# S5 tables moved from GpSimd to VectorE and ScalarE, background PSUM banks behind the LayerNorm lead, epilogue steps moved to VectorE

## The chip, the core and the metric

One core of one Trainium2 chip runs the whole program in one launch. The metric is the device time of one execution in microseconds (us). Before the change three runs took 3293.79, 3299.25 and 3299.61 us; their median is 3299.25 us.

## The reference, cut to what matters

Two decoder blocks of two layers each run one after the other on 256 tokens of width 2048, all in float32:

```python
# block 1
x = LN(ALPHA*x + short_conv_mixer(x))      # w_in 2048x6144, 3-tap causal conv, w_out
x = LN(ALPHA*x + conv_ffn(x))              # w_up 2048x11264, 3-tap conv + bias, silu(g)*u, w_down
x = LN(ALPHA*x + diff_attention(x, k, v))
x = LN(ALPHA*x + conv_ffn(x))
# block 2
h = h + ab_layer(rmsnorm(h))               # dilated attention, gated linear attention
h = h + cd_layer(rmsnorm(h))               # S5 state space layer, gated recurrence
return rmsnorm(h, final_g)

# inside cd_layer, from the parameters alone (no activations):
dt = exp(log_dt); mag = exp(lam_re*dt); ang = lam_im*dt
ab = mag*cos(ang) + 1j*mag*sin(ang)
bb = ((ab - 1)/lam) * b                    # complex; lam, b, c are parameters
# x_t = ab*x_{t-1} + bb u_t ;  y_t = Re(c x_t) + d*u_t
```

The S5 layer is evaluated with tables that depend on the parameters alone (powers of `ab`, rotations, input and output matrices), so they can be made at any time before the last layer.

## The kernel before, in words

**Units.** All weights are streamed from HBM in units of 128 x 1024 numbers (`_units`). For every unit SyncE loads `raw` (3 buffers), ScalarE rounds it to `whi` (`hi_to`, 4 buffers), VectorE makes the rest `wlo = raw - whi` (`lo_to`, 4 buffers), and TensorE multiplies with both halves: 8 matmuls of 512 columns with `whi` (the activations `xs` lie as high and low parts side by side) and 8 of 256 columns with `wlo`. A regular tile of 128 output channels (`mm_tile`) has two units; two units in a row take the halves in turned order (`st["kind"]`), so that the second begins with `wlo`. The result lies in a PSUM bank as two parts of 256 columns.

**Order.** The order of every engine's instructions is written out by the program. `before_unit` emits the load five units ahead and the rounding two ahead; `after_unit` emits `wlo` and then one step of every waiting epilogue (`pending`, `advance`) and of the background generators (`run_bg`): `bg` always, `slow` only while `st["quiet"]` is false. A `yield n` in a background generator lets n units pass. All engines work off their queues in order.

**PSUM.** Three banks with the tag `mm` (pool `pmm`) serve regular tiles, four with the tag `bg` (pool `pbg`) serve background work, one serves statistics. `mm_side` and `mm_lead` work on four tiles at once and take banks of both pools. `merge` frees the bank of a regular tile: ScalarE copies one part to `mt`, and a step later VectorE adds the other (L539).

**Lead.** After a LayerNorm the next product begins before the normalisation is done. `mm_lead` runs two groups of four tiles (16 units) on the unnormalised sum with extra columns: the first group on the four `bg` banks, the second on the three `mm` banks and one `bg` bank. `LayerNorm.apply` (`feed`) meanwhile makes the normalised `hres`, and from it pair after pair of 128-row blocks of `xs`: `high` on ScalarE, `low` on VectorE (L743). What is left of `feed` is emitted in one go behind the lead. The epilogue of a lead tile is `normed`: ScalarE copies four extra columns to `uv`, a step later VectorE adds two of them (L767) and applies mean and deviation (L768, L769), and ScalarE adds the bias. The next regular tile takes the first `mm` bank, which that L768 frees. There are four leads: up of the first FFN, q, up of the second FFN, ab.

**FFN.** `ffn` runs three times an up part (44 pairs of tiles in all) and a down part. The epilogue of an up tile (`epi_up`) merges into `pad`, then `conv3` makes the three taps: the first on ScalarE (an activation with scale and bias), and after a `yield` two on VectorE (L849, L850); then comes SiLU or the product with the gate, and the split into high and low parts.

**Tables.** `s5_tables` is a `slow` generator. GpSimd does nearly all its arithmetic: after a preparation on 32-column rows, eight iterations, each with a table of rotations (36 small operations), a matrix `ba` (six operations of 512 columns), a matrix `ca` (six of 640, one more for the sign, two copies of 512), eight transposes of `ba` on TensorE (tag `bg`, evicted by ScalarE) and 16 matmuls for `s5k`. One iteration's yields add up to 32 units. `LayerNorm.add` sets `quiet` from output tile 4 of the last product on; the end of the lead clears it. `open_b`, in the lead of q, finishes whatever is left.

Of the kernel before, what the change touches and what calls it, by code (L numbers as in the profile page):

```python
# [25 lines left out]
OP = mybir.AluOpType  # L26
# [120 lines left out]
def kernel(ctx: ExitStack, tc: tile.TileContext, A, out, dbg=None, upto=99):  # L147
# [445 lines left out]
    class LayerNorm:  # L593
# [53 lines left out]
        def add(self, m, base):  # L647
# [15 lines left out]
            st["quiet"] = True  # L663
            if m >= 8:
                st["hold"] = True
# [206 lines left out]
    def epi_xv(i):  # L872
        def f(ps):
# [5 lines left out]
            yield from conv3(cur["y", i], pad, [P("a_conv", j * 16 + i) for j in range(3)])  # L879
# [83 lines left out]
    def s5_tables():  # L963
# [7 lines left out]
        def cmul(dr, di, ar, ai, br, bi, eng, u1, u2):  # L971
            eng.tensor_mul(u1, ar, br)
            eng.tensor_mul(u2, ai, bi)
            eng.tensor_sub(dr, u1, u2)
            eng.tensor_mul(u1, ar, bi)
            eng.tensor_mul(u2, ai, br)
            eng.tensor_add(di, u1, u2)
# [10 lines left out]
        G.tensor_mul(abr, mag, cs)  # L988
        G.tensor_mul(abi, mag, sn)
        G.tensor_mul(t1, lr, lr)  # L990
        G.tensor_mul(t2, li, li)
        G.tensor_add(t1, t1, t2)
        yield 4
        V.reciprocal(inv, t1)
        yield 2
        G.tensor_scalar(nr, abr, -1.0, None, op0=OP.add)
        G.tensor_mul(t1, nr, lr)
        G.tensor_mul(t2, abi, li)
        G.tensor_add(t1, t1, t2)
        G.tensor_mul(cor, t1, inv)  # L1000
        G.tensor_mul(t1, abi, lr)
        G.tensor_mul(t2, nr, li)
        G.tensor_sub(t1, t1, t2)
        G.tensor_mul(coi, t1, inv)
        yield 1
        G.tensor_mul(t1, mag, mag)
        G.tensor_mul(mag4, t1, t1)
        G.memset(pa[:, 0, :, 0], 1.0)
        G.memset(pa[:, 1, :, 0], 0.0)
        G.tensor_copy(pa[:, 0, :, 1], abr)  # L1010
        G.tensor_copy(pa[:, 1, :, 1], abi)
        for a, b in ((1, 1), (2, 1), (2, 2)):
            cmul(pa[:, 0, :, a + b], pa[:, 1, :, a + b], pa[:, 0, :, a], pa[:, 1, :, a],
                 pa[:, 0, :, b], pa[:, 1, :, b], G, t1, t2)
        for j in range(4):
            G.tensor_copy(pd[:, :, :, j], pa[:, :, :, 3 - j])
# [3 lines left out]
        cmul(*ph, cs, sn, cs, sn, G, t1, t2)  # L1020
        cmul(pq[:, 0, 0], pq[:, 1, 0], *ph, *ph, G, t1, t2)
        for j in range(5):
            cmul(pq[:, 0, j + 1], pq[:, 1, j + 1], pq[:, 0, j], pq[:, 1, j], pq[:, 0, j], pq[:, 1, j], G, t1, t2)
        yield 1
# [15 lines left out]
        for i in range(8):  # L1040
# [3 lines left out]
            G.tensor_copy(d0[:, :, 1:], mag4[:, p4].unsqueeze(2).to_broadcast([128, 4, 63]))  # L1044
            for k in range(6):
# [3 lines left out]
                cmul(rot[:, 0, :, n:2 * n], rot[:, 1, :, n:2 * n], rot[:, 0, :, :n], rot[:, 1, :, :n],  # L1049
                     fr, fi, G, v1, v2)  # L1050
            yield 3
            cr, ci = (z[:, p4].unsqueeze(2).to_broadcast([128, 4, 16]) for z in (cor, coi))
            w1, w2 = u1[:, :, 0, :16], u2[:, :, 0, :16]
            for r in range(2):
                G.tensor_mul(w1, cr, bc[:, r])
                G.tensor_mul(w2, ci, bc[:, 1 - r])
                for ps_, cs_ in half:
                    (G.tensor_add if r else G.tensor_sub)(bd[ps_, r, :, cs_], w1[ps_], w2[ps_])
# [880 lines left out]
```

## Time and profile before

| | |
|---|---|
| median of three runs | 3299.25 us |
| the profiled execution | 3297.42 us, of which span 3295.6 us |
| mean granted TensorE clock | 0.987 |
| TensorE (PE) busy | 3201.6 us, 97% |
| VectorE (DVE) busy | 2338.4 us, 71% |
| ScalarE (ACT) busy | 1718.4 us, 52% |
| GpSimd (POOL) busy | 827.4 us, 25% |
| DMA | 599.31 MB, mean 182 GB/s |

The span is the time from the first to the last instruction; 1.8 us of the execution lie outside it. Idle time matters on the engine that bounds the kernel, so the page is read together with what ended each wait of that engine. PEclk, the granted clock, is 1.00 at 2.4 GHz and 0.50 at 1.2 GHz.

### The profile page before, as it was taken

The page shows a single profiled execution, that of the slowest core. Times are in us where ns is not written, and L with a number is a line of the kernel's source. Part 1 is how long each engine was busy: PE and PEld are TensorE (multiplying, and loading weights), DVE is VectorE, ACT ScalarE, POOL GpSimd, SP SyncE. Part 2 cuts the span into 40 slices and gives each one's busy share as a digit, 9 for nine tenths or more (in the row PEclk, how much of TensorE's full clock was granted, in tenths as well). Part 3 has the DMA queues.
Part 4 walks back from the last instruction along what each step waited for, and adds up shares of the span by engine and source line. Part 5 has one row for each costly group of instructions (what it writes and reads, how often), then busy time and mean ns, then how long its engine had stood idle before and what let it go on. Part 6 is the DMA issues. An engine that isn't in the chain of part 4 may idle for free.

```text
span 3295.6 us, 51934 instructions
## 1 busy us (share of the span) xinstructions
PE 3201.6 (97%) x18966; PEld 2834.0 (86%) x18966; DVE 2338.4 (71%) x3529; ACT 1718.4 (52%) x2664; POOL 827.4 (25%) x1081
## 2 busy tenths in 40 slices
PE   9989989999999999999999999999989999999998
PEld 8878978788888898887988888888878888899887
DVE  6657886677766787667877676677877666688765
ACT  5544565445545564555655455455564565444754
POOL 4565342455650036241200000000300001121102
PEclk9999999999999999999999999999999999999999
DMA  7656646666656655555556666666544555775454
GB/s 219 195 175 196 189 145 195 185 200 184 202 184 200 187 171 182 158 159 163 171 171 191 188 187 190 191 186 190 163 146 151 161 179 183 226 258 167 151 180 154
DMA packets 258960, 599.31 MB, mean 182 GB/s; under 512 B 38128, under 2 KB 137072, under 8 KB 258704
## 3 DMA queue, kind: packets, MB, share of 16 engines
q1 hardware_dynamic: 256320, 588.38, 58.3%
q0 software_dynamic: 2208, 7.37, 0.7%
q8 instruction: 150, 2.46, 0.3%
q14 instruction: 106, 0.87, 0.1%
q10 hardware_dynamic: 176, 0.23, 0.0%
HBM read 578.04 MB, written 17.83 MB: 181 GB/s over the span
## 4 chain that ended last, share of the span: by engine, by line
PE 73%; DVE 11%; DMA 4%; ACT 4%; issue 3%; POOL 2%; SPq 1%; DVEq 0%; ACTq 0%; POOLq 0%
PE mm L314 43%; PE mm L308 22%; DVE wlo L244 6%; ACT whi L201 3%; DMA raw<-in_cd_dram 1%; PE ml L1383 1%; DVE h L849 1%; SPq L219 1%; DMA raw<-in_up_dram 1%; PE mm L401 1%; PE mm L402 0%; PE mm L400 0%; PE mm L311 0%; PE s5k L1083 0%; DMA raw<-in_ab_dram 0%
## 5 line engine op out<-in xcount | busy, mean ns | idle before, releaser
L244 DVE TENSOR_TENSOR wlo<-raw,whi 128x1024 fp32r<-128x1024 f32 (+3 forms) x1083 | 1366.0, 1264 | 728.8 <-ACT whi L201 700.0
L201 ACT ACTIVATE whi<-raw 128x1024 fp32r<-128x1024 f32 (+3 forms) x1083 | 1119.6, 1038 | 566.0 <-PE mm L314 205.0
L314 PE MATMUL mm<-xs,whi 128*128 128x512 f32 x5264 | 1304.2, 397 | 22.6 <-DVE pad L768 10.4
L314 PEld LDWEIGHTS mm<-xs,whi 128*128 128x128 f32 x5264 | 970.4, 190 | 218.2 <-issue 20.0
L308 PEld LDWEIGHTS mm<-xs,wlo 128*128 128x128 f32 x5264 | 676.5, 190 | 47.3 <-DVE wlo L244 17.6
L308 PE MATMUL mm<-xs,wlo 128*128 128x256 f32 x5264 | 694.6, 283 | 15.2 <-DVE wlo L244 15.1
L314 PE MATMUL mm<-glu,whi 128*128 128x512 f32 x1380 | 343.2, 395 | 9.7 <-DVE pad L539 9.7
L314 PEld LDWEIGHTS mm<-glu,whi 128*128 128x128 f32 x1380 | 253.5, 190 | 58.6 <-issue 11.4
L201 ACT ACTIVATE h<-pad,par 128x256 f32<-128x256 f32 x176 | 104.9, 600 | 328.1 <-DVE pad L539 328.0
L201 ACT ACTIVATE mt<-mm 128x256 f32<-128x256 f32 x337 | 124.9, 371 | 196.8 <-PE mm L314 179.9
L689 POOL TENSOR_TENSOR ln_s<-rf 128x256 f32<-128x256 f32 x2 | 2.1, 1055 | 828.8 <-DVE rf L645 828.8
L308 PEld LDWEIGHTS mm<-glu,wlo 128*128 128x128 f32 x1408 | 188.2, 193 | 17.9 <-DVE wlo L244 7.7
L308 PE MATMUL mm<-glu,wlo 128*128 128x256 f32 x1408 | 192.9, 285 | 6.5 <-DVE wlo L244 6.5
L426 PE MATMUL mm<-xs,wlo 128*128 128x258 f32 (+1 forms) x512 | 145.4, 284 | 4.9 <-DVE wlo L244 4.8
L424 PE MATMUL mm<-xs,whi 128*128 128x260 f32 (+1 forms) x512 | 145.9, 285 | 0.7 <-ACT whi L201 0.5
L428 PE MATMUL mm<-xs,whi 128*128 128x256 f32 (+1 forms) x512 | 144.4, 282 | 0.0
L426 PEld LDWEIGHTS mm<-xs,wlo 128*128 128x128 f32 (+1 forms) x512 | 94.8, 185 | 7.5 <-DVE wlo L244 7.1
L850 DVE SCALAR_TENSOR_TENSOR h<-pad,par,h 128x256 f32<-128x256 f32 x176 | 94.2, 535 | 6.3
L424 PEld LDWEIGHTS mm<-xs,whi 128*128 128x128 f32 (+1 forms) x512 | 94.9, 185 | 1.7 <-ACT whi L201 0.7
L849 DVE SCALAR_TENSOR_TENSOR h<-pad,par,h 128x256 f32<-128x256 f32 x176 | 93.3, 530 | 4.0 <-ACT h L201 4.0
L1091 POOL DMA_DIRECT2D s5b<-s5km x8 | 4.4, 554 | 362.7 <-ACT s5km L201 362.7
L428 PEld LDWEIGHTS mm<-xs,whi 128*128 128x128 f32 (+1 forms) x512 | 94.8, 185 | 0.3
(622 smaller groups left out, 3706.3 us busy)
## 6 DMA issues: line engine op xcount, KB each, us to landing
raw<-in_up_dram SPq DMA_DIRECT2D x320, 512.0 KB, 4.3
raw<-in_ab_dram SPq DMA_DIRECT2D x98, 512.0 KB, 3.9
raw<-in_a_in_dram SPq DMA_DIRECT2D x88, 512.0 KB, 4.5
raw<-in_cd_dram SPq DMA_DIRECT2D x88, 512.0 KB, 4.5
raw<-in_down_dram SPq DMA_DIRECT2D x72, 512.0 KB, 3.8
raw<-in_down_dram SPq DMA_DIRECT2D x168, 128.0 KB, 2.6
raw<-in_down_dram SPq DMA_DIRECT2D x48, 448.0 KB, 4.0
raw<-in_up_dram SPq DMA_DIRECT2D x128, 128.0 KB, 3.1
```

Source lines behind the costliest of these rows:

```text
L201: nc.scalar.activation(dst, src, func, **k)
L219: nc.sync.dma_start(r[:, c:c + nk * m], w[t, :, k0:k0 + nk, :].rearrange("p k n -> p (k n)"))
L244: V.tensor_sub(lo[:, c:c + step], r[:, c:c + step], hi[:, c:c + step].bitcast(F32))
L308: PE.matmul(ps[:m, :T], lo[:, c:c + m], x[:, kx, :T], start=False, stop=last, skip_group_check=True)
L314: PE.matmul(ps[:m, :], hi[:, c:c + m], x[:, kx, :], start=first, stop=last, skip_group_check=True)
L401: PE.matmul(ps[b], xhi, wlo[:, :, k, :], start=False, stop=False, skip_group_check=True)
L424: PE.matmul(p[:, :4 + T], hi[:, w], xt[:, k, PAD - 4:PAD + T], start=k == 0, stop=False, skip_group_check=True)
L426: PE.matmul(p[:, 2:4 + T], lo[:, w], xt[:, k, PAD - 2:PAD + T], start=False, stop=False, skip_group_check=True)
L428: PE.matmul(p[:, 4:4 + T], hi[:, w], xt[:, k, PAD + T:], start=False, stop=k == KT - 1, skip_group_check=True)
L849: V.scalar_tensor_tensor(dst, pad[:, 1:T + 1], w[1], dst, op0=OP.mult, op1=OP.add)
L850: V.scalar_tensor_tensor(dst, pad[:, 2:T + 2], w[2], dst, op0=OP.mult, op1=OP.add)
L1383: PE.matmul(ps[:, 2 * b + hd, :], Kf[:, s], rhs, start=b + hd == 0, stop=b + hd == 2, skip_group_check=True)
```

## The change

Five edits:

1. The first two regular tiles behind each lead take a bank of the background pool instead of one of the three `mm` banks.
2. `normed` reads the extra columns on VectorE straight from PSUM, with one copy and one addition in its first step; the ScalarE copy and a `yield` go.
3. `conv3` makes its first tap on VectorE, and its `yield` goes, so that all three taps follow the merge in one step.
4. The arithmetic of `s5_tables` moves from GpSimd to VectorE, in small steps with a yield behind every one to six operations; plain copies, the sign of `ca` and the two wide copies go to ScalarE. Memsets, the sine arguments and the DMA issues stay on GpSimd. The `ca` part now stands behind the transposes and the write of the first table. One iteration still has 32 units of yields.
5. `quiet` is set from output tile 8 on instead of 4.

The core of the diff:

```diff
-    def mm_tile(x, epi, n_units=2, koff=0, whole=False, now=False):
-        ps = pmm.tile([128, 512], F32, tag="mm", name="mm")
+    def mm_tile(x, epi, n_units=2, koff=0, whole=False, now=False, bank=(pmm, "mm")):
+        ps = bank[0].tile([128, 512], F32, tag=bank[1], name="mm")
...
-        for e in epis[SIDE if ln is None else LEAD * SIDE:]:
-            mm_tile(x, e)
+        for i, e in enumerate(epis[SIDE if ln is None else LEAD * SIDE:]):
+            mm_tile(x, e, bank=(pbg, "bg") if ln is not None and i < 2 else (pmm, "mm"))
...
-            st["quiet"] = True
             if m >= 8:
-                st["hold"] = True
+                st["hold"] = st["quiet"] = True
...
             e = lnp.tile([128, 6], F32, tag="uv", name="uv", bufs=4)
-            S.activation(e[:m, :4], ps[:m, :4], AF.Copy)
-            yield
+            V.tensor_copy(e[:m, :2], ps[:m, :2])
+            V.tensor_add(e[:m, 4:], e[:m, :2], ps[:m, 2:4])
             while not self.ready:
                 yield
-            V.tensor_add(e[:m, 4:], e[:m, :2], e[:m, 2:4])
...
     def conv3(dst, pad, w, bias=0.0):
-        S.activation(dst, pad[:, 0:T], AF.Identity, scale=w[0], bias=bias)
-        yield
+        V.tensor_scalar(dst, pad[:, 0:T], w[0], bias, op0=OP.mult, op1=OP.add)
...
+        def cmul(dr, di, ar, ai, br, bi, u1, u2, n=3):
+            ops = ((V.tensor_mul, u1, ar, br), (V.tensor_mul, u2, ai, bi), (V.tensor_sub, dr, u1, u2),
+                   (V.tensor_mul, u1, ar, bi), (V.tensor_mul, u2, ai, br), (V.tensor_add, di, u1, u2))
+            for i, (f, d, x, y) in enumerate(ops):
+                f(d, x, y)
+                if i % n == n - 1:
+                    yield 1
...
-                cmul(rot[:, 0, :, n:2 * n], rot[:, 1, :, n:2 * n], rot[:, 0, :, :n], rot[:, 1, :, :n],
-                     fr, fi, G, v1, v2)
-            yield 3
+                yield from cmul(rot[:, 0, :, n:2 * n], rot[:, 1, :, n:2 * n], rot[:, 0, :, :n], rot[:, 1, :, :n],
+                                fr, fi, v1, v2, 6 if n < 8 else 3 if n < 16 else 2)
...
-            cmul(ba[:, 0], ba[:, 1], ar, ai, br, bi, G, u1[:, :, :4], u2[:, :, :4])
-            yield 8
-            ar, ai = (pa[:, r, p4].unsqueeze(3).to_broadcast([128, 4, 5, 32]) for r in range(2))
-            br, bi = (cd[:, r].unsqueeze(2).to_broadcast([128, 4, 5, 32]) for r in range(2))
-            cmul(ca[:, 0], ca[:, 1], ar, ai, br, bi, G, u1, u2)
-            G.tensor_scalar(ca[:, 1], ca[:, 1], -1.0, None, op0=OP.mult)
-            for r, u in enumerate((u1, u2)):
-                G.tensor_copy(u[:, :, :4], bd[:, r].unsqueeze(2).to_broadcast([128, 4, 4, 32]))
+            yield from cmul(ba[:, 0], ba[:, 1], ar, ai, br, bi, u1[:, :, :4], u2[:, :, :4], 1)
             for r in range(2):
-                if not r:
-                    yield 2
                 ps = pbg.tile([128, 4, 128], F32, tag="bg", name="s5t")
                 for a in range(4):
                     PE.transpose(ps[:, a, :], ba[:, r, a].rearrange("p j h -> p (j h)"), ident)
                 yield 1
                 S.activation(bt[:, :, r, :], ps, AF.Copy)
             nc.sync.dma_start(s5_a[i], ta)
-            yield 12
+            ar, ai = (pa[:, r, p4].unsqueeze(3).to_broadcast([128, 4, 5, 32]) for r in range(2))
+            br, bi = (cd[:, r].unsqueeze(2).to_broadcast([128, 4, 5, 32]) for r in range(2))
+            yield from cmul(ca[:, 0], ca[:, 1], ar, ai, br, bi, u1, u2, 1)
+            copy(ca[:, 1], ca[:, 1], -1.0)
+            yield 1
+            for r, u in enumerate((u1, u2)):
+                copy(u[:, :, :4], bd[:, r].unsqueeze(2).to_broadcast([128, 4, 4, 32]))
+                yield 1
+            yield 1
             ps = pbg.tile([128, 4, 128], F32, tag="bg", name="s5k")
...
```

`copy` is a ScalarE activation with `AF.Copy`. The preparation's 17 operations and ten complex products on 32 columns, and the eight operations of 64 columns that make `bd` in each iteration, move from `G` to `V` in the same way.

## Rows read from the trace of the kernel before

**Rows 1.** The page, part 1: busy time, share of the span, instructions.
```profile
PE 3201.6 (97%) x18966; PEld 2834.0 (86%) x18966; DVE 2338.4 (71%) x3529; ACT 1718.4 (52%) x2664; POOL 827.4 (25%) x1081
```

**Rows 2.** TensorE's waits, longest first: total us, times, longest us.
```profile
PE mm L308 <- DVE wlo L244: 21.6, 13, 3.4
...
PE mm L314 <- DVE pad L539: 9.7, 4, 4.2
PE s5t L1075 <- POOL s5ba L974: 9.6, 1, 9.6
```

**Rows 3.** The windows view: length, busy us of each engine, clock, DMA.
```profile
442.40:1194.50 752.10, 725.26 (x4144) 635.91 (x4145) 539.11 (x719) 381.80 (x582) 315.63 (x429) 0.98 0.62 188
1655.70:2354.80 699.10, 696.17 (x3984) 611.96 (x3985) 486.69 (x719) 362.25 (x539) 26.89 (x25) 0.99 0.62 185
...
679.70:861.60 181.90, 176.08 (x1010) 154.14 (x1009) 129.43 (x171) 96.50 (x155) 84.03 (x114) 0.98 0.61 188
1867.70:2034.90 167.20, 167.20 (x961) 146.81 (x960) 114.66 (x176) 92.14 (x145) 0.00 (x0) 1.00 0.62 186
```

**Rows 4.** Instructions in order of time, 478 to 486 us: start, duration, wait.
```profile
478.78 1.29 POOL L974 TENSOR_TENSOR s5ba<-s5u,s5u 128x512 f32<-128x512 f32 x1
478.80 2.35 DVE L244 TENSOR_TENSOR wlo<-raw,whi 128x1024 fp32r<-128x1024 f32 x1 [1.68 <-ACT whi L201]
...
481.08 1.27 DVE L849 SCALAR_TENSOR_TENSOR h<-pad,par,h 128x256 f32<-128x256 f32 x1
...
485.80 0.62 PE L308 MATMUL mm<-xs,wlo 128*128 128x256 f32 x3 [3.36 <-DVE wlo L244]
```

**Rows 5.** TensorE's table work by line, 442.4 to 1194.5 us: busy us, mean ns.
```profile
L1083 PE MATMUL s5k<-s5ca,s5u 128*128 128x128 f32 x112 | 13.6, 275 | 0.0
L1075 PE MATMUL s5t<-ident,s5ba 128*128 128x128 f32 x48 | 7.2, 272 | 0.0
```

**Rows 6.** VectorE's groups by line and form: busy us, mean ns.
```profile
L1764 DVE TENSOR_SCALAR hg<-vz,lb 128x256 f32<-128x256 f32 x8 | 3.7, 458 | 0.0
...
L1373 DVE TENSOR_TENSOR qt<-hg 128x512 f32<-128x512 f32 x4 | 2.7, 681 | 0.0
L1765 DVE TENSOR_SCALAR hg<-hg 128x256 f32<-128x256 f32 x8 | 2.7, 337 | 0.6 <-PE m L1402 0.3
L1245 DVE TENSOR_TENSOR sm<-sm,lamf 128x1 f32<-128x1 f32 x16 | 2.5, 156 | 0.3
```

**Rows 7.** TensorE's first regular tile behind each lead, in order of time.
```profile
442.41 3.75 PE L314 MATMUL mm<-xs,whi 128*128 128x512 f32 x8 [5.21 <-DVE pad L768]
...
1249.53 3.75 PE L314 MATMUL mm<-xs,whi 128*128 128x512 f32 x8 [3.94 <-DVE qT L768]
...
1655.68 3.75 PE L314 MATMUL mm<-xs,whi 128*128 128x512 f32 x8 [5.21 <-DVE pad L768]
...
2410.30 3.75 PE L314 MATMUL mm<-xs,whi 128*128 128x512 f32 x8 [4.98 <-DVE vz L768]
```

**Rows 8.** The end of three leads on ScalarE, VectorE and TensorE, in order of time.
```profile
1252.01 1.89 DVE L743 TENSOR_TENSOR xs<-hres,xs 128x512 fp32r<-128x512 f32 x3
...
1643.08 1.57 ACT L201 ACTIVATE h<-pad,par 128x256 f32<-128x256 f32 x3
...
1646.16 1.23 DVE L244 TENSOR_TENSOR wlo<-raw,whi 128x1024 fp32r<-128x1024 f32 x1 [4.09 <-ACT whi L201]
...
1657.62 1.13 ACT L201 ACTIVATE xs<-hres 128x512 fp32r<-128x512 f32 x2
...
1658.84 1.89 DVE L743 TENSOR_TENSOR xs<-hres,xs 128x512 fp32r<-128x512 f32 x3
...
1662.08 3.85 PE L314 MATMUL mm<-xs,whi 128*128 128x512 f32 x16
...
2413.11 2.46 DVE L527 SCALAR_TENSOR_TENSOR xs<-hres,par,xs 128x256 fp32r<-128x256 f32 x6
```

**Rows 9.** The windows view of the stretch behind the wait for `s5ba`.
```profile
197.00:207.30 10.30, 5.77 (x19) 5.00 (x20) 3.01 (x3) 1.54 (x2) 9.85 (x12) 0.50 0.01 3
```

More of the change, by code (lines that the diff above doesn't have):

```diff
@@ L878, in f @@
             cur["y", i] = ep.tile([128, T], F32, tag="c2", name="c2")
-            yield from conv3(cur["y", i], pad, [P("a_conv", j * 16 + i) for j in range(3)])
+            conv3(cur["y", i], pad, [P("a_conv", j * 16 + i) for j in range(3)])
         return f
@@ L969, in s5_tables, with copy @@
         lr, li, ld = P("lam_re", 0, 32), P("lam_im", 0, 32), P("log_dt", 0, 32)
[L971 to L977, printed above, removed]
+        def copy(dst, src, scale=1.0):
+            S.activation(dst, src, AF.Copy, scale=scale)
+        def cmul(dr, di, ar, ai, br, bi, u1, u2, n=3):
[5 more added lines that the diff above has]
+                    yield 1
         yield 20
@@ L987, in s5_tables @@
         yield 1
[L988 to L993, printed above, removed]
-        V.reciprocal(inv, t1)
-        yield 2
[L996 to L1002, printed above, removed]
@@ L1003, in s5_tables @@
-        G.tensor_sub(t1, t1, t2)
-        G.tensor_mul(coi, t1, inv)
-        yield 1
-        G.tensor_mul(t1, mag, mag)
-        G.tensor_mul(mag4, t1, t1)
+        V.tensor_mul(abr, mag, cs)
+        V.tensor_mul(abi, mag, sn)
+        V.tensor_mul(t1, lr, lr)
+        V.tensor_mul(t2, li, li)
+        yield 1
+        V.tensor_add(t1, t1, t2)
+        V.reciprocal(inv, t1)
+        V.tensor_scalar(nr, abr, -1.0, None, op0=OP.add)
+        yield 1
+        V.tensor_mul(t1, nr, lr)
+        V.tensor_mul(t2, abi, li)
@@ L1008, in s5_tables @@
+        V.tensor_add(t1, t1, t2)
+        yield 1
+        V.tensor_mul(cor, t1, inv)
+        V.tensor_mul(t1, abi, lr)
+        V.tensor_mul(t2, nr, li)
+        yield 1
+        V.tensor_sub(t1, t1, t2)
+        V.tensor_mul(coi, t1, inv)
+        yield 1
+        V.tensor_mul(t1, mag, mag)
+        V.tensor_mul(mag4, t1, t1)
         G.memset(pa[:, 0, :, 0], 1.0)
         G.memset(pa[:, 1, :, 0], 0.0)
-        G.tensor_copy(pa[:, 0, :, 1], abr)
-        G.tensor_copy(pa[:, 1, :, 1], abi)
+        copy(pa[:, 0, :, 1], abr)
@@ L1012, in s5_tables @@
+        copy(pa[:, 1, :, 1], abi)
+        yield 1
         for a, b in ((1, 1), (2, 1), (2, 2)):
-            cmul(pa[:, 0, :, a + b], pa[:, 1, :, a + b], pa[:, 0, :, a], pa[:, 1, :, a],
-                 pa[:, 0, :, b], pa[:, 1, :, b], G, t1, t2)
+            yield from cmul(pa[:, 0, :, a + b], pa[:, 1, :, a + b], pa[:, 0, :, a], pa[:, 1, :, a],
+                            pa[:, 0, :, b], pa[:, 1, :, b], t1, t2)
         for j in range(4):
-            G.tensor_copy(pd[:, :, :, j], pa[:, :, :, 3 - j])
+            copy(pd[:, :, :, j], pa[:, :, :, 3 - j])
@@ L1017, in s5_tables @@
         yield 1
         pq = bgp.tile([128, 2, 6, 32], F32, tag="s5pq", name="s5pq", bufs=1)
-        cmul(*ph, cs, sn, cs, sn, G, t1, t2)
-        cmul(pq[:, 0, 0], pq[:, 1, 0], *ph, *ph, G, t1, t2)
+        yield from cmul(*ph, cs, sn, cs, sn, t1, t2)
+        yield from cmul(pq[:, 0, 0], pq[:, 1, 0], *ph, *ph, t1, t2)
         for j in range(5):
-            cmul(pq[:, 0, j + 1], pq[:, 1, j + 1], pq[:, 0, j], pq[:, 1, j], pq[:, 0, j], pq[:, 1, j], G, t1, t2)
-        yield 1
+            yield from cmul(pq[:, 0, j + 1], pq[:, 1, j + 1], pq[:, 0, j], pq[:, 1, j], pq[:, 0, j], pq[:, 1, j],
+                            t1, t2)
@@ L1043, in s5_tables @@
             p4 = slice(4 * i, 4 * i + 4)
-            G.tensor_copy(d0[:, :, 1:], mag4[:, p4].unsqueeze(2).to_broadcast([128, 4, 63]))
+            copy(d0[:, :, 1:], mag4[:, p4].unsqueeze(2).to_broadcast([128, 4, 63]))
             for k in range(6):
@@ L1078, in s5_tables @@
             nc.sync.dma_start(s5_a[i], ta)
-            yield 12
+            ar, ai = (pa[:, r, p4].unsqueeze(3).to_broadcast([128, 4, 5, 32]) for r in range(2))
+            br, bi = (cd[:, r].unsqueeze(2).to_broadcast([128, 4, 5, 32]) for r in range(2))
+            yield from cmul(ca[:, 0], ca[:, 1], ar, ai, br, bi, u1, u2, 1)
+            copy(ca[:, 1], ca[:, 1], -1.0)
+            yield 1
+            for r, u in enumerate((u1, u2)):
+                copy(u[:, :, :4], bd[:, r].unsqueeze(2).to_broadcast([128, 4, 4, 32]))
+                yield 1
+            yield 1
             ps = pbg.tile([128, 4, 128], F32, tag="bg", name="s5k")
@@ L1091, in s5_tables @@
             nc.gpsimd.dma_start(s5_b[i][:, 1024:], km.rearrange("p a c -> p (a c)"))
-            yield 4
+            yield 1
     spawn(masks(), slow)
@@ L1133, in f @@
                     h = ep.tile([128, T], F32, tag=f"c{is_u}", name="h")
-                    yield from conv3(h, pad, [P("f_conv", (layer * 3 + q) * 88 + j) for q in range(3)],
+                    conv3(h, pad, [P("f_conv", (layer * 3 + q) * 88 + j) for q in range(3)],
                           P("f_convb", layer * 88 + j))
```

10 lines of the change are left out of this document (5 added, 5 removed).

## The prediction

> **What bounds the kernel now.** The page's busy times come first: TensorE is busy 97% of the span, VectorE 71% [rows 1]. So time can come from three places only: what TensorE waits for, what it does at the lower clock, and work of its own. The view of TensorE's waits is next: most often it waits for `wlo`, which VectorE makes; next come merges that free PSUM banks, and one long wait for a matrix that GpSimd makes [rows 2]. The waits behind the leads are read one by one in the timeline [rows 7]. The windows view then shows where `wlo` is late. The two FFNs run the same code on other weights; the first takes 752.1 us and the second 699.1 us. GpSimd is busy 315.6 us in the first and 26.9 us in the second, and VectorE needs 539.1 us against 486.7 us for the same operations [rows 3]. The timeline shows why: while GpSimd works on 512-column operands, a `wlo` takes 2.35 us (1.23 us with GpSimd idle) and a tap 1.27 us, and TensorE then waits 3.36 us for the next `wlo` [rows 4, 8]. The tables, hidden on GpSimd as it seems, are paid for by VectorE and so by TensorE.
>
> **The change, part by part.** All sums are made against the profiled execution, 3297.4 us (span 3295.6 and 1.8 outside), which lies 1.8 us under the median of 3299.25.
>
> *1. The a_in part.* The transposes of the first iteration wait 9.6 us for GpSimd [rows 2], and TensorE's queue is in order, so everything waits. The 10.3 us behind run at 1.2 GHz with TensorE busy for 5.8 us [rows 9], half of which, 2.9 us, is lost. Now VectorE makes `ba` one operation per unit and the transposes come a unit later. Both losses should go, 12.5 us; the lower end is none, if the transposes meet another late operand. I take 12.
>
> *2. GpSimd's contention in the first FFN.* The FFNs differ by 53.0 us [rows 3]. The first also holds 160 of the 192 table matmuls and transposes, 13.6 + 7.2 = 20.8 us of TensorE [rows 5], which stay. That leaves 32.2 us.
>
> Whether all of it comes back depends on VectorE, which gets the tables. Prices are a line between 156 ns for 1 column and 681 ns for 512 [rows 6]: about 189 ns for 32 columns, 222 for 64, 287 for 128, 812 for 640. One iteration: 36 rotation operations, six each of 4, 8, 16, 32, 64 and 128 columns, 7.2 us; eight of 64 columns 1.8; six of 512 4.1; six of 640 4.9; together 18.0 us. Eight iterations are 144 us, and 77 operations of the preparation at 189 ns are 14.6 us. The first FFN gets 160/192 of the iterations, 120 us, and 84 first taps. A tap took 458 ns with two column operands, as here, and 337 ns with constants [rows 6]; start to start less, so I take 410 ns, 34 us. The Trainium skill ("VectorE: DVE Perf Modes", Mode 2×_2P) says that a float32 tensor-scalar operation from SBUF to SBUF can make two results per cycle; an estimate by it is some 200 ns a tap, 17 us here in place of 34, which would leave VectorE more room. The two rows lie above it.
>
> VectorE's demand in the first FFN is thus 486.7 + 34 + 120 = 641 us, in 699.1 + 20.8 = 720 us: 89%. The up parts are fuller. The middle one: 114.7 us in 167.2 us without tables [rows 3], plus 30 taps (12.3 us) and 60 units at 18.0/32 = 0.56 us (33.8 us) gives 161 of some 173 us, 93%. In six units of an iteration a 640-column operation comes each time, and demand goes a little above 100%; `wlo` has some two units (5.6 us) of lead, which covers that. The first up part begins with the lead's backlog and gets no air. So I take 26 of the 32.2 us. Ends: all 32.2 with `wlo` always in time; 5 if VectorE is late in every up part.
>
> What covers the moved work elsewhere: ScalarE gives up the 192 first taps and gets the copies, a few per iteration, so it has room. GpSimd's queue loses the arithmetic ahead of its DMA issues; SyncE's write of the first table comes earlier in the iteration, behind the same eviction. New waits are VectorE's for ScalarE's copies of `ab` and for the matmuls that read `u1` and `u2`; behind them stand `wlo` and merges, and TensorE waits for those. They are emitted a unit or more behind what they wait for: between 0 and 2.8 us (a unit) per iteration; I take 0.
>
> *3. The leads.* TensorE waits 5.21, 3.94, 5.21 and 4.98 us for the first regular tile's bank, and its first eight matmuls then take 3.75 us [rows 7] where 16 take 3.85 us at full clock [rows 8]: 1.8 us more each. Together 19.3 + 7.3 = 26.6 us. With a `bg` bank the tile starts at once. What is late next: the second unit needs the last `xs` blocks, and these are still to be made. In the lead of the second FFN ScalarE makes them at 1657.62 and VectorE ends at 1658.84 + 1.89 = 1660.7 us [rows 8], while TensorE, free from 1650.5, would need them by about 1653.4. Some of this moves forward: three first taps leave ScalarE (1.57 us), and they and the taps behind them fill VectorE's wait of 4.09 us for `whi` [rows 8]. I take 2.5 us earlier, so the last block at 1658.2 and the second unit's end a last 1 us behind. Before it ended at 1662.08 + 1.92 = 1664.0. That gains 4.8 us. In the first FFN the tables resume there; I take 3. In q and ab nothing moves forward: the last blocks end at 1252.01 + 1.89 = 1253.9 and 2413.11 + 2.46 = 2415.6 [rows 8], 4.4 and 5.3 us after TensorE's restart [rows 7]; the second unit ended some 8.3 us after the restart, as in the second FFN. Less the last 1 us, that leaves 2.9 and about 2.0; I take 2.6 and 2.6. Sum 13. Ends: 0 (the `xs` blocks later by the two VectorE reads in `normed`) and 26.6.
>
> *4. Taps and `normed`.* A merge is no longer behind the previous tile's two taps on VectorE, as these follow their own merge. This bears on the waits for merges, 9.7 us in four [rows 2], of which all but the second FFN's is in part 2 already. That FFN has 2.9 us of idle in all [rows 3], and a wait costs some slow matmuls. I take 2 (between -3, if the taps make `wlo` late there, and 4). VectorE is at 69% there.
>
> *5. Costs.* `quiet` from tile 8 on puts some eight units of tables into the first LayerNorm's load on VectorE: at 0.56 us, 4.5 us of work, of which I charge 1.
>
> Sum: 12 + 26 + 13 + 2 - 1 = 52 us, and 3297.4 - 52 = 3245 us, 1.6% under the median.
>
> **The rivals.**
>
> *A, everything comes back:* 12.5 + 32.2 + 26.6 + 4 = 75 us, 3222 us. For it: VectorE's demand stays under 100% in every part. Against it: the late `xs` blocks behind the leads, which the change does not touch.
>
> *B, a wait takes the place of another:* behind the leads TensorE waits as long for `xs` as it did for the bank (0 to 3 us gained), and the first FFN gets only half (16 us), since its up parts are now short of VectorE in place of GpSimd's contention. With 10 us from the a_in part that is 26 to 29 us: 3270 us. For it: 93% demand and an order that cannot be changed once it is written.
>
> *C, slower: VectorE becomes the bound of the first FFN.* All 120 us of tables stand in queue between `wlo` and merges. If an operation costs f times my price, demand is 521 + 120 f. It fills the 720 us at f = 1.66, reaches the 752 us of before at f = 1.93, and eats the other gains (27 us) too at f = 2.15. At f = 2.4 the FFN takes 809 us: 3297 + 57 - 27 = 3327 us. For it: the operands are strided and broadcast, and dependent chains of operations of 4 to 32 columns leave gaps between them. Against it: 150 ns is already the price of one column, all fixed cost, and half of the sum is 512 and 640 columns wide. The Trainium skill ("Perfetto Trace Analysis", Optimizing Scalar/DVE Operations) advises the other direction: when VectorE is saturated, hand work to ScalarE or even GpSimd. VectorE is the busier of the two here (71% to 52%), and by that rule this rival or B should win; the same passage warns that VectorE and GpSimd share a read port, and the FFN rows show that half of it.
>
> *D, the change doesn't do what it says:* the two `bg` banks are not free. The rotation gives the tile behind the lead the bank of a tile of the first group, read some eight units earlier, so I hold it unlikely; then the leads gain nothing, about 3258 us.
>
> **How the numbers follow.** Forecast 0.52, A 0.17, B 0.19, C 0.07, D 0.05. The likeliest is 3245 us. 8 times in 10: from 3210 (A, and some merges more) to 3280 (B with a part of its gains lost). A change within 0.2% (6.6 us) cannot be told from none. Faster by more: forecast, A, D and nearly all of B, 0.89. Within: 0.04, from between B and C. Slower: 0.07, C.
>
> **What would show it.** In the changed profile GpSimd has little to do before 1000 us; `wlo` has one duration, about 1.22 us, throughout; the wait for `s5ba` and the slow stretch behind it are gone; the first FFN is at most some 727 us long, about 700 + 21 + 6. Behind each lead the wait for L768 is gone and a shorter one, for `xs`, stands one unit later. VectorE's busy time rises to some 2520 us (2338 + 159 tables + 79 taps - 52 of contention). I am wrong if TensorE's waits for `wlo` in the first FFN are longer in sum than before, if the leads lose nothing or everything, or if VectorE's 512-column operations take far more than 0.68 us.

## The result, and the profile after

The median fell from 3296.52 us (3293.78 to 3299.61, four runs) to 3255.20 us (3253.52 to 3259.09, four runs): ratio 0.9876, 95% interval 0.9859 to 0.9893. The profiled execution took 3254.82 us, 3253.0 of it span, against a span of 3295.6 before: 42.6 us less, where the sum said 52.

The page of the changed kernel, part 1 (busy us, share, instructions), answers [rows 1]. VectorE took 153 us more, GpSimd 393 us less, TensorE 13 us less for the same instructions:

```profile
PE 3188.4 (98%) x18966; PEld 2822.9 (87%) x18966; DVE 2491.8 (77%) x4277; ACT 1663.7 (51%) x2510; POOL 434.8 (13%) x487
```

TensorE's waits after the change (total us, times, longest) answer [rows 2]. The wait for `s5ba` is gone and the other two of [rows 2] are shorter. But L426, the lead's own matmul, waits 11.9 us where it waited 4.8, and the waits for L742 and L814, work that follows a LayerNorm, are new.

```profile
PE mm L426 <- DVE wlo L244: 11.9, 9, 3.3
PE mm L308 <- DVE wlo L244: 7.8, 14, 1.2
...
PE st L821 <- DVE rms_s L814: 5.3, 1, 5.3
PE mm L314 <- DVE xs L742: 5.0, 5, 1.9
...
PE mm L314 <- DVE pad L539: 2.3, 1, 2.3
```

The windows view over the first FFN, the second, and the middle up part of each (columns as in [rows 3]): the first FFN lost 30 us, though VectorE works 79 us more in it; the second is as long as before.

```profile
433.64:1155.70 722.06, 713.86 (x4155) 627.34 (x4154) 618.38 (x1151) 369.30 (x550) 41.24 (x46) 1.00 0.64 198
1615.70:2314.50 698.80, 695.28 (x3988) 610.67 (x3987) 529.72 (x810) 330.16 (x457) 28.22 (x26) 1.00 0.62 186
656.00:828.00 172.00, 172.00 (x1010) 151.58 (x1009) 153.37 (x310) 90.93 (x142) 3.07 (x5) 1.00 0.64 201
1827.70:1995.00 167.30, 167.30 (x962) 146.90 (x961) 129.35 (x205) 80.64 (x117) 0.00 (x0) 1.00 0.61 188
```

`wlo` there takes 1.22 us at the median and never more than 1.76 (min/median/max in ns), where [rows 4] had one of 2.35, and VectorE's new operations (busy us, mean ns) have the prices that were read off [rows 6]:

```profile
L244 DVE TENSOR_TENSOR wlo<-raw,whi x255: 687/1220/1762, 435.9 to 1155.8; 128x1024 fp32r<-128x1024 f32 x116, 128x768 fp32r<-128x768 f32 x12
```
```profile
L845 DVE TENSOR_SCALAR h<-pad,par 128x256 f32<-128x256 f32 x84 | 35.1, 418 | 2.7
L976 DVE TENSOR_TENSOR s5u<-s5pa,s5cd 128x640 f32<-128x640 f32 x28 | 22.9, 819 | 0.0
L976 DVE TENSOR_TENSOR s5u<-s5pd,s5bd 128x512 f32<-128x512 f32 x26 | 17.8, 685 | 0.0
```

Behind the leads the first regular tile starts at once and its eight matmuls run at full clock, as the timeline of the second FFN shows beside [rows 7]. The next unit then waits for `xs` on both engines, its second eight matmuls come late and at half the pace. The last `xs` block ends 9.1 us behind the start of the lead's last matmul, where in [rows 8] it ended 10.5 behind:

```profile
1615.68 2.00 PE L314 MATMUL mm<-xs,whi 128*128 128x512 f32 x8
...
1620.11 1.02 PE L308 MATMUL mm<-xs,wlo 128*128 128x256 f32 x4 [1.01 <-ACT xs L201]
...
1622.78 1.89 DVE L742 TENSOR_TENSOR xs<-hres,xs 128x512 fp32r<-128x512 f32 x3
...
1623.52 3.78 PE L314 MATMUL mm<-xs,whi 128*128 128x512 f32 x8 [1.92 <-DVE xs L742]
```

By stages, worked out from the first and last matmul of each (us):

```
                                       before   after   difference   forecast
a_in part                               289.3   278.3      -11.0        -12
y_conv part                              91.3    93.9       +2.6         +1
first FFN, regular tiles                752.1   722.0      -30.1        -26
four leads, to the first regular tile   219.8   211.4       -8.4  \
what follows leads 2, 3 and 4                              +9.6   /     -13
second FFN, first down part              87.5    83.8       -3.7         -2
rest                                                        -1.6
```

So all large terms came near their size but one: the leads gave nothing (-8.4 and +9.6). And the largest came for a reason that the prediction did not have.

### The profile page after: what moved, and what is told of

It is laid out like the page before. It is cut to its first block, busy times and chain, and to the rows that moved or that the text cites. A ratio compares the mean times of both kernels' runs of the same rounds, so it can differ in the third digit from the quotient of the medians.

```text
span 3253.0 us, 51907 instructions
## 1 busy us (share of the span) xinstructions
PE 3188.4 (98%) x18966; PEld 2822.9 (87%) x18966; DVE 2491.8 (77%) x4277; ACT 1663.7 (51%) x2510; POOL 434.8 (13%) x487
## 4 chain that ended last, share of the span: by engine, by line
PE 81%; DVE 10%; DMA 4%; ACT 2%; issue 2%; SPq 1%; POOL 0%; DVEq 0%; ACTq 0%
PE mm L314 48%; PE mm L308 25%; DVE wlo L244 4%; ACT whi L201 1%; PE ml L1386 1%; DMA raw<-in_up_dram 1%; SPq L219 1%; DMA raw<-in_ab_dram 1%; DMA raw<-in_a_in_dram 1%; PE mm L311 1%; DVE xs L527 1%; DMA raw<-in_v_dram 1%; DMA raw<-in_q_dram 1%; PE mm L401 1%; PE mm L402 0%
## 5 line engine op out<-in xcount | busy, mean ns | idle before, releaser
L244 DVE TENSOR_TENSOR wlo<-raw,whi 128x1024 fp32r<-128x1024 f32 (+3 forms) x1083 | 1329.3, 1230 | 519.4 <-ACT whi L201 487.0
L314 PE MATMUL mm<-xs,whi 128*128 128x512 f32 x5264 | 1296.0, 395 | 12.2 <-DVE xs L525 6.0
L314 PEld LDWEIGHTS mm<-xs,whi 128*128 128x128 f32 x5264 | 962.4, 189 | 206.9 <-DVE xs L525 8.4
L314 PE MATMUL mm<-glu,whi 128*128 128x512 f32 x1380 | 338.6, 392 | 2.3 <-DVE pad L539 2.3
L314 PEld LDWEIGHTS mm<-glu,whi 128*128 128x128 f32 x1380 | 251.1, 188 | 49.5 <-ACT s5ca L201 2.7
L426 PE MATMUL mm<-xs,wlo 128*128 128x258 f32 (+1 forms) x512 | 148.3, 290 | 11.9 <-DVE wlo L244 11.9
L426 PEld LDWEIGHTS mm<-xs,wlo 128*128 128x128 f32 (+1 forms) x512 | 97.5, 190 | 14.6 <-DVE wlo L244 14.0
L1092 POOL DMA_DIRECT2D s5b<-s5ca x8 | 7.3, 909 | 694.0 <-ACT s5ca L201 694.0
L201 ACT ACTIVATE h<-h 128x256 f32<-128x256 f32 x88 | 36.7, 417 | 121.0 <-DVE h L847 120.9
L847 DVE SCALAR_TENSOR_TENSOR h<-pad,par,h 128x256 f32<-128x256 f32 x176 | 85.4, 485 | 6.3
L846 DVE SCALAR_TENSOR_TENSOR h<-pad,par,h 128x256 f32<-128x256 f32 x176 | 85.3, 485 | 6.2
```

Source lines behind the costliest of these rows:

```text
L201: nc.scalar.activation(dst, src, func, **k)
L244: V.tensor_sub(lo[:, c:c + step], r[:, c:c + step], hi[:, c:c + step].bitcast(F32))
L314: PE.matmul(ps[:m, :], hi[:, c:c + m], x[:, kx, :], start=first, stop=last, skip_group_check=True)
L426: PE.matmul(p[:, 2:4 + T], lo[:, w], xt[:, k, PAD - 2:PAD + T], start=False, stop=False, skip_group_check=True)
L846: V.scalar_tensor_tensor(dst, pad[:, 1:T + 1], w[1], dst, op0=OP.mult, op1=OP.add)
L847: V.scalar_tensor_tensor(dst, pad[:, 2:T + 2], w[2], dst, op0=OP.mult, op1=OP.add)
```

## Experiments

### The first FFN: tables and taps one by one

*tables_only*, the kernel before with the table edit alone:

```diff
-        G.tensor_mul(abr, mag, cs)
+        V.tensor_mul(abr, mag, cs)
...
-            cmul(ba[:, 0], ba[:, 1], ar, ai, br, bi, G, u1[:, :, :4], u2[:, :, :4])
-            yield 8
+            yield from cmul(ba[:, 0], ba[:, 1], ar, ai, br, bi, u1[:, :, :4], u2[:, :, :4], 1)
```

> The kernel before with edit 4 alone: the table arithmetic on VectorE and ScalarE in small steps, everything else as before. Theory (the gain is GpSimd's contention with VectorE, and the other edits cancel): about 3256 us; the first FFN some 722 us long in place of 752, the a_in part 11 us shorter, the four waits behind the leads unchanged at 4 to 5 us each. Rival (the gain comes from the lead, bank and tap edits): over 3280 us, the first FFN over 740 us.

Measured: 3282.99 us, ratio 0.9968 (0.9956 to 0.9981). The a_in part lost 14 us; the first FFN stayed at 753.0. GpSimd's contention was gone from it and nothing came back. The rival's numbers came, and so fell the step that explained the 30 us by contention alone.

*taps_back*, the changed kernel with the old taps:

```diff
-        V.tensor_scalar(dst, pad[:, 0:T], w[0], bias, op0=OP.mult, op1=OP.add)
+        S.activation(dst, pad[:, 0:T], AF.Identity, scale=w[0], bias=bias)
+        yield
...
-                    conv3(h, pad, [P("f_conv", (layer * 3 + q) * 88 + j) for q in range(3)],
+                    yield from conv3(h, pad, [P("f_conv", (layer * 3 + q) * 88 + j) for q in range(3)],
...
```

> The changed kernel with edit 3 undone: first taps on ScalarE with the yield, the rest as changed. Theory 1: 3250 to 3256 us; the 3.3 us waits for wlo inside the two FFN leads shrink below 1.5 us, but the waits for merges between up and down come back with some 2 us each. Theory 2: about 3245 us, the leads 10 us shorter in sum.

Measured: 3288.19 us, 0.9982 (0.9972 to 0.9991), first FFN 758.5. The edit that the prediction priced at 2 us is worth 33 beside tables on VectorE; no theory had expected that. TensorE waited 42 times for `wlo`, at most 1.7 us each.

*taps_only*, the kernel before with that edit alone (its reverse, as above):

> The kernel before with the tap edit alone: the first tap on VectorE, nothing yielded before it; the tables stay on GpSimd. Theory (round trip): a tap on ScalarE stands between VectorE's merge and the rounding of the next unit (whi), so each delay of VectorE's queue comes back to VectorE as a late whi; without that trip the first FFN gains a part although GpSimd still slows VectorE: first FFN 735 to 745 us of 752, VectorE's idle time for whi in the middle up part (660 to 840 us) falls from 45 to under 20 us, total 3280 to 3290. Rival (contention, as predicted): the FFN's loss is GpSimd's and VectorE gets 34 us more work, so the first FFN stays at 752 or gets longer, total 3294 to 3305.

Measured: 3273.23 us, 0.9924 (0.9912 to 0.9937), first FFN 727.9: more than the theory asked for, with GpSimd still at work for 324 us of it. VectorE's idle time for `whi` from 660 to 840 us fell from 44.9 to 21.6 us, a little short of what it asked for.

*tables_taps*, the two together without the rest:

> The kernel before with the table edit and the tap edit, without the lead edits and with quiet as before. Theory: these two make the whole gain together, first FFN about 722, total 3253 to 3258, though each alone is worth little (tables 3283). Rival: the lead's banks, the normed reads or quiet are needed too, total 3262 to 3275.

Measured: 3249.84 us, 0.9858 (0.9843 to 0.9873), first FFN 719.3. The two edits make the whole gain; the other three together add nothing that can be told (0.9876 with them, and the intervals overlap).

*before_notab* and *after_notab* leave out the table arithmetic of iterations 1 to 7:

```diff
-                cmul(rot[:, 0, :, n:2 * n], rot[:, 1, :, n:2 * n], rot[:, 0, :, :n], rot[:, 1, :, :n],
+                if i == 0:
+                    cmul(rot[:, 0, :, n:2 * n], rot[:, 1, :, n:2 * n], rot[:, 0, :, :n], rot[:, 1, :, :n],
```

> The kernel before; leaves out GpSimd's table arithmetic of iterations 1 to 7 (iteration 0, the transposes, table matmuls, ScalarE's copies and the DMAs stay). The first FFN is then the second FFN plus the table matmuls. Theory (the loss belongs to the tables, on whichever of the two engines, as long as the taps go through ScalarE): first FFN 718 to 726 us of 752, total 3262 to 3270. Rival (the round trip of the taps costs its share by itself): first FFN over 735 us, total 3278 to 3292.

> The changed kernel; leaves out VectorE's table arithmetic of iterations 1 to 7 (the steps, transposes, table matmuls, ScalarE's copies and the DMAs stay). Theory (with the taps on VectorE the table operations fall into time in which VectorE was idle): first FFN 714 to 722 of 722, total 3246 to 3256. Rival (some 100 us of table operations on VectorE still cost TensorE): first FFN under 712 us, total 3230 to 3244.

Measured: 3257.15 us, 0.9880 (0.9863 to 0.9896), first FFN 713.4; and 3248.23 us, 0.9849 (0.9834 to 0.9863), first FFN 715.4. The first is a little under what was expected, total and FFN; the second is within. With the others this fills a table (first FFN, us):

```
tables              none    on GpSimd    on VectorE
taps as before     713.4      752.1        753.0
taps as changed    715.4      727.9        722.0
```

Read it by rows. With the old taps the tables cost 39 to 40 us on either engine; with the new ones 12 on GpSimd and 7 on VectorE. Without tables the taps hardly matter (2.0 us). The cells do not all come from one kernel: 715.4 and 722.0 have edits 1, 2 and 5 too. With the tables on VectorE, *tables_taps* (new taps, without those edits) gives 719.3 and *taps_back* (old taps, with them) gives 758.5, so the reading holds on either base. Contention is real: VectorE takes 539.1 us for its work before and 485.8 us in *before_notab*, for the same 719 instructions. The windows view of *before_notab*, the first FFN:

```profile
438.24:1151.60 713.36, 711.50 (x4146) 627.18 (x4146) 485.79 (x719) 384.68 (x582) 40.10 (x45) 1.00 0.66 198
```

But these 53 us on VectorE, like the table operations that replace them, are a load on its queue, and it is the old order of the taps that hands such a load on to TensorE.

How it does so can be followed in the waits view from 660 to 840 us, most of which is the middle up part in every kernel; here VectorE's and ScalarE's longest in *tables_only*:

```profile
DVE wlo L244 <- ACT whi L201: 41.2, 33, 2.2
```
```profile
ACT h L201 <- DVE pad L539: 64.8, 25, 3.5
```

and the same of the changed kernel, where ScalarE waits for weights and for finished taps instead:

```profile
DVE wlo L244 <- ACT whi L201: 13.8, 9, 4.4
```
```profile
ACT whi L201 <- DMA raw<-in_up_dram: 24.8, 30, 2.0
ACT h L201 <- DVE h L847: 22.8, 14, 2.7
```

In *tables_only* the two engines wait for each other. Such waits are no loss by themselves: *before_notab* has as many of them, and TensorE waits for nothing in its middle up part (655.2 to 827.4 us):

```profile
DVE wlo L244 <- ACT whi L201: 57.3, 31, 3.7
```
```profile
ACT h L201 <- DVE pad L539: 54.4, 28, 2.8
```

There VectorE is busy for 114.7 us of the part. In *tables_only* it has 138.0 us of work in it (658.0 to 839.6 us) and still waits 41.2 us for `whi`. TensorE then waits 11 times for `wlo`, 6.1 us in sum, and the part is 181.6 us long and not 172.2. The timeline of *tables_only* shows one round (start us, us; in brackets the idle time before and what ended it):

```profile
742.52 0.42 DVE L539 TENSOR_TENSOR pad<-mm,mt 128x256 f32<-128x256 f32 x1
742.85 0.68 DVE L979 TENSOR_TENSOR s5ba<-s5u,s5u 128x512 f32<-128x512 f32 x1
742.97 0.60 ACT L201 ACTIVATE h<-pad,par 128x256 f32<-128x256 f32 x1 [3.40 <-DVE pad L539]
743.48 1.04 ACT L201 ACTIVATE whi<-raw 128x1024 fp32r<-128x1024 f32 x1
...
744.56 1.23 DVE L244 TENSOR_TENSOR wlo<-raw,whi 128x1024 fp32r<-128x1024 f32 x1 [1.02 <-ACT whi L201]
...
745.70 0.48 DVE L849 SCALAR_TENSOR_TENSOR h<-pad,par,h 128x256 f32<-128x256 f32 x1
746.22 0.49 DVE L850 SCALAR_TENSOR_TENSOR h<-pad,par,h 128x256 f32<-128x256 f32 x1
746.62 0.68 DVE L979 TENSOR_TENSOR s5u<-s5pd,s5bd 128x512 f32<-128x512 f32 x1
...
747.22 1.22 DVE L244 TENSOR_TENSOR wlo<-raw,whi 128x1024 fp32r<-128x1024 f32 x1
...
748.50 1.21 PE L308 MATMUL mm<-xs,wlo 128*128 128x256 f32 x8 [0.34 <-DVE wlo L244]
```

ScalarE's tap waits 3.40 us for the merge on VectorE, and the rounding of the next unit (`whi`) stands behind it. VectorE, out of work, then waits 1.02 us for that `whi`. The two other taps had what they needed from 743.6 on, but they are issued a step later, behind `wlo`; so VectorE idles first and is late afterwards. The next `wlo` ends at 748.44, and TensorE has waited 0.34 us for it. In the changed kernel the merge, the three taps, a table operation and `wlo` follow each other on VectorE with no gap:

```profile
707.41 0.42 DVE L539 TENSOR_TENSOR pad<-mm,mt 128x256 f32<-128x256 f32 x1
707.86 0.41 DVE L845 TENSOR_SCALAR h<-pad,par 128x256 f32<-128x256 f32 x1
...
708.31 0.49 DVE L846 SCALAR_TENSOR_TENSOR h<-pad,par,h 128x256 f32<-128x256 f32 x1
708.84 0.49 DVE L847 SCALAR_TENSOR_TENSOR h<-pad,par,h 128x256 f32<-128x256 f32 x1
709.24 0.69 DVE L976 TENSOR_TENSOR s5u<-s5pd,s5bd 128x512 f32<-128x512 f32 x1
709.84 1.22 DVE L244 TENSOR_TENSOR wlo<-raw,whi 128x1024 fp32r<-128x1024 f32 x1
```

### Which half of the tap edit does it: the engine or the step

*tap_act_now* and *tap_dve_yield*, the changed kernel with one half of the tap edit undone each:

```diff
# tap_act_now
-        V.tensor_scalar(dst, pad[:, 0:T], w[0], bias, op0=OP.mult, op1=OP.add)
+        S.activation(dst, pad[:, 0:T], AF.Identity, scale=w[0], bias=bias)
# tap_dve_yield (with yield from conv3(...) at both calls)
         V.tensor_scalar(dst, pad[:, 0:T], w[0], bias, op0=OP.mult, op1=OP.add)
+        yield
```

> The changed kernel with the first tap on ScalarE again, but issued at once behind the merge and not a step later. Theory (round trip through ScalarE): whi queues behind a tap that waits for VectorE's merge, so it is as slow as with the old taps: first FFN 750 to 760, ScalarE waits over 40 us for pad in the middle up part, total 3280 to 3290. Rival (the order of the steps: the taps come one unit earlier): first FFN about 722 and total 3253 to 3260 whichever engine makes the tap.

> The changed kernel with the first tap on VectorE, but the two further taps a step later, as with the old taps. Theory (round trip): no trip through ScalarE, so it keeps the gain: first FFN 720 to 728, total 3253 to 3262. Rival (the order of the steps): 3280 to 3290, as with the old taps.

Measured: 3260.66 us, 0.9888 (0.9874 to 0.9901), and 3243.35 us, 0.9831 (0.9818 to 0.9845). First FFN, us:

```
first tap on     two further taps a step later    at once
ScalarE                     758.5                  732.4
VectorE                     718.5                  722.0
```

Neither theory had it. The trip through ScalarE alone costs 10 us, the later step alone nothing (it gains 3.6); both together cost 36. *tap_act_now* still has the trip: ScalarE waits 52.8 us for `pad` from 660 to 840 us, near the 64.8 of *tables_only*. But there VectorE waits some 0.7 us for each first tap and then has the two other taps to do while ScalarE rounds (in one round from 744.05 and 743.93 us on). For `whi` it waits 13.6 us in sum, where *tables_only* had 41.2:

```profile
DVE h L846 <- ACT h L201: 18.8, 28, 0.7
DVE wlo L244 <- ACT whi L201: 13.6, 10, 5.1
```

*tap_dve_yield* is also faster than the changed kernel, its span 10.3 us shorter: 3.6 in the first FFN, 3.4 in the a_in part, whose epilogues have such taps too, and 3.7 in the first lead. What makes the 3.6 us in the FFN is not shown.

### The leads

*banks_back* is the changed kernel with `mm` banks behind the lead, *banks_normed* the kernel before with the edits of banks and `normed` alone:

```diff
# banks_back (banks_normed has the reverse, and the new normed)
-        for i, e in enumerate(epis[SIDE if ln is None else LEAD * SIDE:]):
-            mm_tile(x, e, bank=(pbg, "bg") if ln is not None and i < 2 else (pmm, "mm"))
+        for e in epis[SIDE if ln is None else LEAD * SIDE:]:
+            mm_tile(x, e)
```

> The changed kernel with edit 1 undone: the first regular tiles behind the leads on mm banks again. Theory 1: 3255 to 3262 us; waits of 3 to 5 us for the bank come back behind each lead, and the waits for xs (5.0 us in sum) and for the statistics (5.3 us) go. If the bank edit is worth what was forecast for it, over 3265 us.

> The kernel before with edits 1 and 2 alone: background banks behind the leads, and normed on VectorE; tables on GpSimd, first taps on ScalarE. Theory 1 (the wait for the bank is replaced by one for the last xs blocks and the statistics, whatever the taps do): 3290 to 3297 us, the four waits for L768 gone and waits for xs of 2 to 3 us in their place. Theory 2 (the leads would have gained the 13 us of the forecast and the taps took it back): about 3283 us, no wait over 1.5 us inside the two FFN leads.

Measured: 3255.69 us, 0.9883 (0.9870 to 0.9897); and 3297.98 us, 1.0011 (1.0002 to 1.0020). In *banks_normed* the four waits for L768 (19.3 us) are gone, and in their place stand 5.8 us for `xs`, 5.3 us for the statistics and 8.3 us more for `wlo`. In *banks_back* waits for the bank come back, though only the one in the lead of ab at its old length (5.1 us; 0.9 to 1.6 us in the others), and the one for the statistics goes. So the waits go and come with the edit, and the time does not. The reads of `normed` were not tried by themselves.

*xs_first* is *tap_dve_yield* with the last `xs` blocks issued ahead of the epilogues of the second lead group, and the RmsNorm sum of the ab stage put off by two steps more:

```diff
+                    if g == LEAD - 1:
+                        for _ in feed:
+                            pass
                     gens = [e((p, ln)) for e, p in zip(epis[g * SIDE:], ps)]
...
             self.tail.append(self.rstd)
-            yield
+            for _ in range(3):
+                yield
```

> The kernel of tap_dve_yield (3243), with the last LayerNorm steps (the last xs blocks) issued ahead of the normed epilogues of the second lead group, and the RmsNorm sum of the ab stage issued three units later. Theory (the bank was one of two conditions: behind the lead the second unit needs the last xs blocks, which stand in the queues behind the second group's epilogues): now the freed banks are worth something, the waits for xs behind the leads (2.7, 1.8, 2.7 us) and for the statistics (5.3 us) go, total 3230 to 3237. Rival (VectorE and ScalarE have a fixed amount of work behind a lead, and what is put back only moves the wait, to wlo or to the next merge): the same waits in sum, total 3241 to 3248.

Measured: 3247.85 us, 0.9861 (0.9845 to 0.9877), no faster than *tap_dve_yield*. The rival's number came. TensorE's waits behind the second FFN's lead, *tap_dve_yield* and then *xs_first*:

```profile
PE mm L308 <- ACT xs L201: 2.7, 1, 2.7
PE mm L308 <- DVE wlo L244: 1.9, 1, 1.9
```
```profile
PE mm L308 <- DVE wlo L244: 5.3, 2, 4.9
```

Where the time comes back shows in the times of the first 64 L314 matmuls behind that lead, counted from the lead's start (us, the end of the n-th):

```
n                    1      8     16     24     32     64
before             55.0   58.0   62.6   64.5   68.2   79.3
after              53.8   55.4   64.2   67.3   71.1   82.1
tap_dve_yield      48.9   50.5   57.8   59.7   66.9   78.3
xs_first           48.9   50.5   54.2   56.1   67.5   78.6
```

*xs_first* is 8.4 us ahead of before at the 24th matmul and 0.7 us ahead at the 32nd and 64th. In the last two orders of the table VectorE is all but full there: from the lead's end to the 64th matmul it is busy for 28.5 of 29.7 us in *tap_dve_yield* and for 28.9 of 30.0 in *xs_first*, with the last `xs` blocks, four `normed` epilogues, the taps of the lead's tiles, and `wlo`. What is put first puts the rest back. That the wait for the bank, too, was only the place where TensorE paid for such work fits *banks_normed*, but is argued: in the kernel before, VectorE is busy for 25.8 of 30.2 us in that stretch. Summed over the four leads, the 64th matmul comes after 324.3 us before, 327.4 after, 325.4 in *tap_dve_yield* and 320.4 in *xs_first*, whose lead ab lost its 5.3 us (L821) and got a wait of 5.0 us for `arena` further on (1.4 in *tap_dve_yield*).

The changed kernel's row also shows a cost: its lead is 4.9 us longer than *tap_dve_yield*'s. The timeline of the changed kernel has three triples of taps, nine operations in 4.2 us, in one step ahead of `wlo` (first and last shown):

```profile
1601.87 0.41 DVE L845 TENSOR_SCALAR h<-pad,par 128x256 f32<-128x256 f32 x1
...
1605.56 0.48 DVE L847 SCALAR_TENSOR_TENSOR h<-pad,par,h 128x256 f32<-128x256 f32 x1
...
1607.16 1.22 DVE L244 TENSOR_TENSOR wlo<-raw,whi 128x1024 fp32r<-128x1024 f32 x1
```

TensorE waits 3.3 us for that `wlo`, the longest of the L426 waits above. In *tap_dve_yield*, with the taps spread over two steps, TensorE waits 0.4 us in that lead.

### quiet

*quiet_back*, *tap_dve_yield* with `quiet` from tile 4 on as before:

```diff
+            st["quiet"] = True
             if m >= 8:
-                st["hold"] = st["quiet"] = True
+                st["hold"] = True
```

> The kernel of tap_dve_yield (3243), with quiet set from tile 4 on as before the change. Theory (the later quiet puts table work into the first LayerNorm's load on VectorE): y_conv returns from 94.0 to 91.8 us, total 3240 to 3243. Rival (the table steps are only put off and cost the same later, in the first up part, which is full): y_conv shorter, the up part longer by as much, total 3243 to 3247.

Measured: 3234.82 us (3233.39 to 3236.44), 0.9819 (0.9804 to 0.9833). The y_conv part went from 94.0 to 91.8, the first lead from 51.6 to 48.6, the first up part from 133.9 to 133.2, so nothing was only put off. The total lies under both ranges. Against *tap_dve_yield* the total is too close to tell (the intervals overlap). But this kernel beats both of the comparison: the one before by 1.8%, the changed one by 0.6%, with intervals that lie apart.

## Why the prediction was right, and where not

*The a_in part (12):* right, 11. The wait is gone, and the place of the slow stretch [rows 9] runs at the high clock with no idle time (the row below). That stretch began before the wait ended (at 201.5 us), so its 10.3 us did not all lie behind it, but its 5.8 us of busy time did. The transposes do not come a unit later but at 258.8 us, where they came at 201.5, and behind them too TensorE is busy throughout at clock 1.00 (258.8 to 269.1 us):

```profile
200.00:210.00 10.00, 10.00 (x60) 8.85 (x59) 8.19 (x24) 5.50 (x8) 0.00 (x0) 1.00 0.59 179
```

*The first FFN (26 of 32.2):* near in size, wrong in cause, and so near by luck. The sum gave the 26 us to the table move and nothing here to the taps; alone, the table move is worth nothing in this FFN and the tap edit 24 us. "Whether all of it comes back depends on VectorE" was the right question, asked of its busy time alone: demand was put at 641 of 720 us (618 measured), and the old taps and the new differed in the sum only by 34 us of load. But it is not by its load that the tap edit counts: it breaks up a ring of waits between two engines, neither of which is full (VectorE 78% busy, ScalarE 53%, in the first FFN of *tables_only*). Without it the same table move gives nothing in the FFN. The rows were there, though they do not say by themselves what such waits cost. In the kernel before, too, VectorE and ScalarE waited for each other from 660 to 840 us, and I had read the waits view for TensorE only:

```profile
DVE wlo L244 <- ACT whi L201: 44.9, 30, 3.4
```
```profile
ACT h L201 <- DVE pad L539: 58.0, 24, 6.2
```

What could be recovered was 38.7 us (752.1 to 713.4), not 32.2. Of these, 25.0 are idle time of TensorE and 13.8 are slower matmuls (725.3 us busy in [rows 3], 711.5 in *before_notab*).

By the Trainium skill ("Perfetto Trace Analysis", Optimizing Scalar/DVE Operations) moving some work off VectorE may make sense if VectorE is saturated. Here that condition was not met, before the change (539 of 752 us busy in the first FFN) or after it (618 of 722), so the passage gave no ground for rivals B and C, and work put on VectorE paid. The passage's other sentence, that GpSimd and VectorE share a read port, agrees with the 539.1 and 485.8 us above; that the port is what slowed VectorE, no run here shows.

*The leads (13):* the step that failed. They gave -8.4 and +9.6 us, so nothing, and "if the leads lose nothing or everything" was one of the prediction's own signs of being wrong. "I take 2.5 us earlier, so the last block at 1658.2": measured from the start of the lead's last matmul, VectorE's last block ended 9.1 us behind it after the change (1624.67 us) and 10.5 before, 1.4 us earlier and not 2.5. And the lead itself took 53.3 us to its last matmul, where it took 48.8. (For q and ab the working gives 2.9 and 2.0 us, and 2.6 each was taken; that is small beside it.) What failed is what was left out. The freed time was read off the next late operand alone, `xs`, and not off all that VectorE and ScalarE still had to do in that stretch; and the taps, which were to fill a wait there, made a later `wlo` late. Rival B had this half of it: a wait takes the place of another. Rival D's time, 3258 us, came nearest to the 3255 measured, but not by its reason: the banks were free, the waits for L768 are gone, and the leads still gained nothing.

*Taps and merges (2):* in the second FFN 3.7, all of it in the first down part, which began with a wait of 1.9 us for a merge and now has none. What the tap edit is worth beside tables on VectorE, the 33 us of *taps_back*, the prediction had nowhere. *quiet (1):* 2.6 in the y_conv part; *quiet_back* has 2.3 of them from it, and 3.0 in the first lead that were not foreseen.

VectorE's busy time of 2520 us came out at 2491.8. Rival C needed operations at 1.66 times the price; the wide ones cost 1.01 to 1.05 times (685 and 713 to 681 ns), the narrow ones at most 1.16 times (220 to 189). Its other ground, chains with gaps, did not come either: VectorE's idle time in front of the table operations is under 1 us in sum in every group of them.

## What to carry to other kernels

Where two in-order engines hand a tile to and fro, look at the waits of both, and not only at how full each is. That each waits mostly for the other is no loss by itself, but a load on one of them can then reach the third engine although neither is full: here the tables cost 39 to 40 us with the old taps and 7 to 12 with the new. One operation moved to the fuller engine gained more here than the move of a helper's whole work (24 us and nothing in the first FFN). Give the trip's idle time something to do (issue what depends on it at once) or take the trip out. Before a wait on the bound engine is costed as a gain, add up everything its feeders still have to do in that stretch, since the wait may be only the place where that is paid.

## What the hardware showed that was not expected

Broadcast operands cost VectorE next to nothing: 512 and 640 columns took 685 and 819 ns, where plain rows gave 681 and, extended by a line, 812. The first tap, with two column operands, took 418 ns: not the 458 of the nearest row, and not the some 200 of the prediction's estimate. And GpSimd's work made the same 719 VectorE operations 53 us longer; with the tables on GpSimd the first FFN lost 39 us in the old kernel, and 12 with the taps changed.
